# Residual rows of three layer norms and low parts of five weight blocks moved from GpSimd to VectorE, and a selection cut into ten steps

## The chip, the cores and the metric

One core of one Trainium2 chip. The metric is the device time of one execution in microseconds (us), the median of several runs. Engines are named as the profile names them: PE (TensorE matmul), PEld (its weight loads), DVE (VectorE), ACT (ScalarE), POOL (GpSimd), SP (SyncE, which issues all the loads of weights here).

## The reference, cut to what matters

The program runs four transformer layers on 256 tokens of width 1024, all in float32. Layers 0 and 1 (sparse attention, retention, MLP) are not touched by the change. Layers 2 and 3 use post-layer-norm:

```python
def second_block(x, ...):
    for i in range(DEPTH):                     # DEPTH = 2
        h = mixer_sb_ssm(x, ...) if i % 2 == 0 else mixer_dsa(x, ...)
        x = layer_norm(ALPHA * x + h, ln_mix_g[i], ln_mix_b[i])
        x = layer_norm(ALPHA * x + sq_relu_mlp(x, mlp_w1[i], mlp_w2[i]), ln_ffn_g[i], ln_ffn_b[i])

def layer_norm(x, g, b):
    y = (x - mean(x)) * rsqrt(var(x) + 1e-5) * g + b

def mixer_dsa(x, w_in, w_out):                 # "sparse attention" below
    q, k, v, qi, ki, wi = split(x @ w_in)
    score = einsum(relu(qi . ki), wi)          # 8 index heads of 32
    score = where(causal, score, -inf)
    idx = top_k(score, 64)                     # per query
    ... softmax attention over the 64 chosen keys, 16 heads of 64, ALiBi slopes
    return o @ w_out
```

There are four layer norms in layers 2 and 3. The last one writes the output and has other code; the other three are called norm 1 (after the mixer of layer 2), norm 2 (after the MLP of layer 2) and norm 3 (after the sparse attention of layer 3).

## The kernel before, in words

**Split products.** Each float32 product is made of three matmuls: weights and activations are split into a high part (rounded) and a low part (`lo = x - hi`), and `mm3` (lines 378 to 383) sums hi·hi, hi·lo and lo·hi. Weights come in units, one after the other in the list of `_sequence` (line 233), each as two halves of 128x1024 elements a partition row block. For each half SP issues the load into a `raw` buffer, ACT writes `hi` (line 357), and DVE or POOL writes `lo` (line 359): `_split` gives the first `POOL[name]` halves of a unit to POOL and the rest to DVE. `raw`, `hi` and `lo` have five buffers each; in layers 2 and 3 a unit is split one unit ahead of its use.

**The order of the work.** The body is Python that traces instructions in program order. When the kernel is built, a scheduler with its own model of times puts each engine's instructions in a fixed order: of those that are ready in the model, the one traced first goes first. `behind` (line 293) forces what is traced in its block to stand behind given instructions on the same engine, without waiting for their end. Side work is written as generators: `e.add` puts one in a list, and each `yield` of the main work calls `e.step` (line 303), which runs each side generator by one step. So the place of a `yield` decides between which pieces of the main work a piece of side work is traced.

**The layer norm** (`_LayerNorm`). Tokens lie in two tiles T = 0, 1 of 128, columns in two halves. `half` (line 505) makes statistics; `turn` (line 553) transposes the normalised rows on PE, ACT applies gain and bias (line 1576), and `cut` (line 1582) makes the high part on DVE (line 1589) and the low part on POOL for T = 0 (line 1594) and on DVE for T = 1 (line 1591). The next matmuls need these `ah` and `al` tiles. `finish` (line 1601) then traces the residual rows: the normalised activation in row layout, gain and bias applied, which is added again much later (line 1516 in the next norm, or line 2010 in the sparse attention's output). Three quarters of it are made in `finish` on POOL (lines 1611 and 1612): for T = 0 all 1024 columns, for T = 1 the second 512.

**The MLP** (`_mlp`, line 1232) follows norms 1 and 3. Products `f1(c)` (48 matmuls) and the rows of `f2(c)` alternate; for each c, DVE has four `lo`, one square (line 1241) and one low part (line 442).

**The sparse attention** (`_dsa`, line 1874) follows norm 2. In program order: units dki, dqi, dv 0, dv 1 (index keys, index queries, values and index weights), then dk and dq 0 to 3 (keys, queries), of eight k-tiles each; each of these gives two `yield`s. After dk, `put_k` (line 1921) and after each dq, `put_q` (line 1928) copy the result out of PSUM on ACT and DVE (DVE: lines 1926 and 1936). All ten halves of dk and dq have their `lo` on POOL. Side work `side_index` (line 1891) begins at the first yield of dk: it makes the scores of 8 index heads (matmuls line 1896, relu on ACT line 1898, two multiply-adds on DVE line 1902), then eight passes of line 1908 (the eight largest) and line 1910 (strike them out), then the mask `dm` (lines 1912 and 1913), all traced in one step. After it come 18 steps of `_attention` (line 717): `stage_a` (scores on PE lines 743 and 744, DVE line 1956, ACT line 1959, DVE lines 1961 and 1964), `stage_b` (transposes line 1971, ACT line 1973), `stage_c` (line 1985, and low parts at line 442). A step waits until the dq it needs has been traced. In this kernel seven of these steps are traced between the dq units. The output product `do` (96 matmuls of 512 columns) starts once two pairs of heads are done and is interleaved with the rest of the attention; it is completed inside norm 3's `last_rows` (line 1424).

Of the kernel before, what the change touches and what calls it, by code (L numbers as in the profile page):

```python
# [12 lines left out]
ALU = mybir.AluOpType  # L13
# [247 lines left out]
class _Env:  # L261
    BUFS = {"raw": 5, "hi": 5, "lo": 5, "ah": 8, "al": 8, "b8": 5, "b4": 7, "b2": 12, "b1": 7, "sm": 24, "s16": 32,
            "rc": 2}
    AHEAD, LOAD = 2, 4
    POOL = {"dk": 2, "dq": 2, "rv": 1, "rg": 1, "ma": 1, "mb": 1, "up": 1, "su": 1, "glu": 1, "sv": 1, "ksw": 1}

    def __init__(self, ctx, tc, ws):
        self.tc, self.nc, self.ws = tc, tc.nc, ws
        self.pools = {}
        self.ctx = ctx  # L270
        self.ps = {k: ctx.enter_context(tc.tile_pool(name="ps" + k, bufs=4, space=PSUM)) for k in "aw"}
        self.table, _ = _offsets()
        self.seq = _sequence()
        self.pos = {k: n for n, k in enumerate(self.seq)}
        self.raws, self.parts = {}, {}
        self.loaded = self.cut = 0
        self.n = 0
        self.side = []
        self.after = ()
    def t(self, tag, shape, dt=F32):  # L280
        if tag not in self.pools:
            self.pools[tag] = self.ctx.enter_context(
# [19 lines left out]

    def step(self):
        for item in list(self.side):
            with self.behind(item[1]):
                over = next(item[0], self) is self
            if over:
                self.side.remove(item)
# [130 lines left out]
def _hilo(e, hi, lo, src):  # L439

    return (e.nc.scalar.activation(out=hi, in_=src, func=AF.Copy),  # L441
            e.nc.vector.tensor_tensor(out=lo, in0=src, in1=hi.bitcast(F32), op=ALU.subtract))  # L442
# [30 lines left out]
class _Norm(_Act):  # L473
# [8 lines left out]
    def slice(self, xT, c):  # L482
        self.add(xT[:, 2 * c:2 * c + 2], self.g[:, 2 * c:2 * c + 2])
        if c == 0:
            self.e.after = self.last
        self.square(xT, c)
# [745 lines left out]
def _mlp(e, i, act, rows, late=lambda: None):  # L1232

    nc = e.nc
    rels = {}

    def f1(c):
        def emit(_, bank):
            r = e.t("b2", [128, 2, 256])
            nc.scalar.activation(out=r, in_=bank, func=AF.Relu)  # L1240
            nc.vector.tensor_tensor(out=r, in0=r, in1=r, op=ALU.mult)
            h = e.t("b2", [128, 2, 256], F32R)
            l = e.t("b2", [128, 2, 256], F32R)
            _hilo(e, h, l, r)
            rels[c] = ([h[:, 0], h[:, 1]], [l[:, 0], l[:, 1]])
        e.run(e.transposed(("f1", i, c), act, emit, kind="w"))

    e.AHEAD = 1
    f1(0)
    for c in range(13):  # L1250
        f1(c + 1)
        e.run(rows((c,), (rels.pop(c),)))
    late()
    f1(14)
    f1(15)
    e.run(rows((13, 14, 15), (rels[13], rels[14], rels[15])))
# [231 lines left out]
class _LayerNorm:  # L1488

    def __init__(self, e, K, lncol, ln, out, xn, which, i, final):
        self.e, self.K, self.xn, self.final, self.out = e, K, xn, final, out
        self.gb = []
        for v in range(2):
            t = e.t("b4", [128, 1024])
            row = 4 * which + 2 * v + i
            e.nc.sync.dma_start(out=t, in_=ln[row:row + 1, :].to_broadcast([128, 1024]))
            self.gb.append(t)
        self.gc, self.bc = (lncol[:, 8 * (4 * which + 2 * v + i):8 * (4 * which + 2 * v + i) + 8] for v in range(2))  # L1500
        self.xo = e.t("b8", [128, 2, 1024])
        self.v, self.st, self.src = [], [], []
        self.hi, self.lo = [], []
# [49 lines left out]
    def turn(self, T):  # L1553
# [7 lines left out]
        for h in range(2):  # L1561
# [17 lines left out]
            if T == 1:  # L1579
                self.cut(T, h)  # L1580

    def cut(self, T, h):
        e, V, G = self.e, self.e.nc.vector, self.e.nc.gpsimd
        ts = slice(128 * T, 128 * T + 128)
        y = self.y.pop((T, h))
        for n in range(2):
            q = 2 * h + n
            hi, lo = self.hi[q][:, :, ts], self.lo[q][:, :, ts]
            V.tensor_copy(out=hi, in_=y[:, 2 * n:2 * n + 2])  # L1589
            if T:  # L1590
                self.vlast = V.tensor_tensor(out=lo, in0=y[:, 2 * n:2 * n + 2], in1=hi.bitcast(F32), op=ALU.subtract)  # L1591
            else:
                with e.behind((self.pow,)):
                    self.glast = G.tensor_tensor(out=lo, in0=y[:, 2 * n:2 * n + 2], in1=hi.bitcast(F32),
                                                 op=ALU.subtract)
# [5 lines left out]
    def finish(self):  # L1601
        if self.final:
            return
        e, G = self.e, self.e.nc.gpsimd
        self.cut(0, 1)
        e.warm(6, (e.mlast,))
        self.turn(1)
        e.after = (self.alast, self.vlast)
        with e.behind((self.glast,)):
            for T, c in ((0, slice(0, 1024)), (1, slice(512, 1024))):  # L1610
                G.tensor_tensor(out=self.xo[:, T, c], in0=self.v[T][:, c], in1=self.gb[0][:, c], op=ALU.mult)
                G.tensor_tensor(out=self.xo[:, T, c], in0=self.xo[:, T, c], in1=self.gb[1][:, c], op=ALU.add)  # L1612
        l2 = lambda ts: [t[:, k] for t in ts for k in range(2)]
        return self.xo, (l2(self.hi), l2(self.lo))

# [258 lines left out]
def _dsa(e, act, C, ident, mask1, l2, acc, ai, xn):  # L1874
# [16 lines left out]
    def side_index():  # L1891
        for h in range(8):
            hs = slice(32 * (h % 4), 32 * (h % 4) + 32)
            ps = e.bank()
            for T, (o, n) in enumerate(span):
                PE.matmul(out=ps[:, o:o + n], lhsT=qi[hs, h // 4, 128 * T:128 * T + 128], rhs=ki[hs, :n])
            r = e.t("b2", [128, 384])
            A.activation(out=r, in_=ps[:, :384], func=AF.Relu)
            for T, (o, n) in enumerate(span):
                sl = slice(o, o + n)  # L1900
                prev = mask1[:, 256 - n:] if h == 0 else idx[:, sl]
                V.scalar_tensor_tensor(out=idx[:, sl], in0=r[:, sl], scalar=vw[:, T, 256 + h:257 + h], in1=prev,  # L1902
                                       op0=ALU.mult, op1=ALU.add)
        for it in range(8):
            src = work if it else idx
            m8 = [e.t("sm", [128, 8]) for _ in range(2)]
            for T, (o, n) in enumerate(span):
                V.max(out=m8[T], in_=src[:, o:o + n])
            for T, (o, n) in enumerate(span):
                V.match_replace(out=work[:, o:o + n], in_to_replace=m8[T], in_values=src[:, o:o + n],  # L1910
                                imm_value=-3e38)
        V.tensor_tensor(out=dm, in0=work, in1=idx, op=ALU.is_equal)
        V.scalar_tensor_tensor(out=dm, in0=dm, scalar=FAR, in1=C["negd"], op0=ALU.mult, op1=ALU.add)
        yield from _attention(e, 16, stage_a, stage_b, stage_c, 2, lambda s: len(queries) > min(s, 15) // 4)
# [128 lines left out]
```

## Time and profile before

| what | value |
|---|---|
| median of 3 runs | 1530.6 us (1530.14 to 1534.49) |
| the profiled execution, its own time | 1529.34 us |
| its span, first to last instruction | 1527.6 us |
| PE busy | 1460.5 us, 96% of the span |
| DVE busy | 1057.9 us, 69% |
| ACT busy | 772.6 us, 51% |
| POOL busy | 382.2 us, 25% |
| granted PE clock, mean | 0.98 of 2.4 GHz |

How to read it: the busy time of an engine is summed over records; matmuls are pipelined, so their records overlap. PE is the engine to watch: a stretch costs time where PE is idle, or where its granted clock is 0.5 (1.2 GHz in place of 2.4). An idle PE shows in the trace as a wait in square brackets in front of a matmul, with the instruction that ended it. Norm 1 lies at 1020 to 1024 us of the span, norm 2 at 1209 to 1216, norm 3 at 1330 to 1335, the sparse attention between the last two.

### The profile page before, as it was taken

The page shows a single profiled execution, that of the slowest core. Times are in us where ns is not written, and L with a number is a line of the kernel's source. Part 1 is how long each engine was busy: PE and PEld are TensorE (multiplying, and loading weights), DVE is VectorE, ACT ScalarE, POOL GpSimd, SP SyncE. Part 2 cuts the span into 40 slices and gives each one's busy share as a digit, 9 for nine tenths or more (in the row PEclk, how much of TensorE's full clock was granted, in tenths as well). Part 3 has the DMA queues.
Part 4 walks back from the last instruction along what each step waited for, and adds up shares of the span by engine and source line. Part 5 has one row for each costly group of instructions (what it writes and reads, how often), then busy time and mean ns, then how long its engine had stood idle before and what let it go on. Part 6 is the DMA issues. An engine that isn't in the chain of part 4 may idle for free.

```text
span 1527.6 us, 26445 instructions
## 1 busy us (share of the span) xinstructions
PE 1460.5 (96%) x10596; PEld 1334.1 (87%) x10596; DVE 1057.9 (69%) x1628; ACT 772.6 (51%) x1192; POOL 382.2 (25%) x274
## 2 busy tenths in 40 slices
PE   7999999999989999988999999999999888999997
PEld 6868999999988789988999998778999787789997
DVE  7687768555688786699755778876555669675556
ACT  5555445444546554453544555464444447644442
POOL 4353314000144433158200237520000251110000
PEclk8999999999999999998999999999999999999999
DMA  7553455555455554533655453236555352255551
GB/s 247 198 171 119 148 187 166 194 184 188 161 154 196 189 173 139 184 133 125 202 170 186 156 177 125 97 124 206 188 186 189 108 187 97 97 180 191 185 189 69
DMA packets 70682, 250.75 MB, mean 164 GB/s; under 512 B 8096, under 2 KB 8480, under 8 KB 70560
## 3 DMA queue, kind: packets, MB, share of 16 engines
q1 hardware_dynamic: 70560, 249.07, 49.1%
q8 instruction: 83, 1.36, 0.4%
q14 instruction: 39, 0.32, 0.1%
HBM read 247.99 MB, written 1.05 MB: 163 GB/s over the span
## 4 chain that ended last, share of the span: by engine, by line
PE 77%; DVE 13%; issue 3%; ACT 2%; DMA 2%; POOL 1%; DVEq 0%; SPq 0%; ACTq 0%; POOLq 0%
PE psa L382 14%; PE psa L381 14%; PE psa L383 14%; PE psw L382 9%; PE psw L383 9%; PE psw L381 9%; DVE lo L359 3%; DMA raw<-in_ws_dram 2%; DVE al L462 1%; ACT hi L357 1%; DVE al L1591 1%; PE psw L1057 1%; DVE b L1902 1%; DVE b L1851 1%; DVE b L1031 1%
## 5 line engine op out<-in xcount | busy, mean ns | idle before, releaser
L359 DVE TENSOR_TENSOR lo<-raw,hi 128x1024 fp32r<-128x1024 f32 (+2 forms) x397 | 504.3, 1279 | 324.9 <-ACT hi L357 324.5
L357 ACT ACTIVATE hi<-raw 128x1024 fp32r<-128x1024 f32 (+1 forms) x448 | 465.2, 1045 | 505.4 <-PE psw L382 207.1
L382 PE MATMUL psw<-al,hi 128*128 128x256 f32 x1152 | 328.4, 285 | 6.6 <-DVE al L1591 5.5
L383 PE MATMUL psw<-ah,lo 128*128 128x256 f32 x1152 | 328.2, 285 | 3.0 <-DVE lo L359 2.8
L381 PE MATMUL psw<-ah,hi 128*128 128x256 f32 x1152 | 328.0, 285 | 0.0
L382 PEld LDWEIGHTS psw<-al,hi 128*128 128x128 f32 x1152 | 222.8, 193 | 9.2 <-POOL b L1612 4.6
L383 PEld LDWEIGHTS psw<-ah,lo 128*128 128x128 f32 x1152 | 222.7, 193 | 4.1 <-DVE lo L359 4.0
L381 PEld LDWEIGHTS psw<-ah,hi 128*128 128x128 f32 x1152 | 222.5, 193 | 1.1
L382 PE MATMUL psa<-b,hi 128*128 128x256 f32 x640 | 182.4, 286 | 8.5 <-DVE b L442 8.5
L383 PE MATMUL psa<-b,lo 128*128 128x256 f32 x640 | 181.8, 285 | 0.0
L381 PE MATMUL psa<-b,hi 128*128 128x256 f32 x640 | 180.4, 286 | 0.6 <-ACT b L441 0.6
L359 POOL TENSOR_TENSOR lo<-raw,hi 128x1024 fp32r<-128x1024 f32 x51 | 125.1, 2457 | 210.6 <-ACT hi L357 192.2
L381 PE MATMUL psa<-ah,hi 128*128 128x256 f32 x456 | 133.7, 294 | 1.5 <-DVE ah L1589 1.5
L382 PE MATMUL psa<-al,hi 128*128 128x256 f32 x456 | 132.1, 290 | 2.0 <-DVE al L1591 2.0
L383 PE MATMUL psa<-ah,lo 128*128 128x256 f32 x456 | 132.6, 291 | 0.0
L382 PEld LDWEIGHTS psa<-b,hi 128*128 128x128 f32 x640 | 124.1, 194 | 9.3 <-DVE b L442 9.2
L382 PE MATMUL psa<-lo,ah 128*128 128x512 f32 (+2 forms) x320 | 123.1, 387 | 8.1 <-DVE lo L359 7.1
L383 PEld LDWEIGHTS psa<-b,lo 128*128 128x128 f32 x640 | 124.2, 194 | 0.0
L381 PE MATMUL psa<-hi,ah 128*128 128x512 f32 (+2 forms) x320 | 123.5, 394 | 0.5 <-ACT ah L1412 0.4
L381 PEld LDWEIGHTS psa<-b,hi 128*128 128x128 f32 x640 | 123.0, 194 | 1.0 <-ACT b L441 0.9
L383 PE MATMUL psa<-hi,al 128*128 128x512 f32 (+2 forms) x320 | 119.6, 386 | 1.2 <-DVE al L462 1.2
L1526 POOL TENSOR_TENSOR sm<-sm,mhalf 128x1 f32<-128x1 f32 x8 | 5.8, 722 | 449.7 <-DVE sm L1525 445.2
(352 smaller groups left out, 2753.6 us busy)
## 6 DMA issues: line engine op xcount, KB each, us to landing
raw<-in_ws_dram SPq DMA_DIRECT2D x450, 512.0 KB, 4.2
b<-in_ln_dram SPq DMA_DIRECT2D x8, 512.0 KB, 5.1
raw<-in_ws_dram SPq DMA_DIRECT2D x8, 280.0 KB, 4.3
raw<-in_ws_dram SPq DMA_DIRECT2D x4, 264.0 KB, 2.7
b<-in_x_dram SPq DMA_DIRECT2D x4, 256.0 KB, 5.1
out_dram<-b SPq DMA_DIRECT2D x4, 256.0 KB, 2.0
cb<-in_cb_dram SPq DMA_DIRECT2D x1, 676.0 KB, 7.5
b<-in_p_dram SPq DMA_DIRECT2D x2, 256.0 KB, 5.1
```

Source lines behind the costliest of these rows:

```text
L357: self.nc.scalar.activation(out=hi, in_=w, func=AF.Copy)
L359: eng.tensor_tensor(out=lo, in0=w, in1=hi.bitcast(F32), op=ALU.subtract)
L381: mm(out=out, lhsT=lh, rhs=rh, start=start, stop=False, skip_group_check=shared)
L382: mm(out=out, lhsT=lh, rhs=rl, start=False, stop=False, skip_group_check=shared)
L383: self.mlast = mm(out=out, lhsT=ll, rhs=rh, start=False, stop=stop, skip_group_check=shared)
L462: v = e.nc.vector.scalar_tensor_tensor(out=l[:, k], in0=srcs[:, k], scalar=g, in1=h[:, k].bitcast(F32), op0=ALU.mult, op1=ALU.subtract)
L1031: V.tensor_scalar(out=sb[:, o:o + n], in0=sb[:, o:o + n], scalar1=sm[:, T:T + 1], scalar2=None, op0=ALU.mult)
L1057: PE.matmul(out=o[64 * gg:64 * gg + 64, q0:256], lhsT=kvn[:, kt, v0:v0 + 64], rhs=pts[s - 2 + 2 * gg][:, 256 * kt:256 * kt + 256 - q0], st ...
L1526: self.glast = self.pow = G.tensor_tensor(out=r, in0=r, in1=self.K["mhalf"][:, :1], op=ALU.pow)
L1591: self.vlast = V.tensor_tensor(out=lo, in0=y[:, 2 * n:2 * n + 2], in1=hi.bitcast(F32), op=ALU.subtract)
L1851: V.tensor_tensor_scan(out=xs[:, q, c], data0=mt[:, q], data1=w[:, q, c], initial=0.0, op0=ALU.mult, op1=ALU.add)
L1902: V.scalar_tensor_tensor(out=idx[:, sl], in0=r[:, sl], scalar=vw[:, T, 256 + h:257 + h], in1=prev, op0=ALU.mult, op1=ALU.add)
```

## The change

Three parts:

1. The `lo` of dk (2 halves) and dq (8 halves) is made on DVE: `dk` and `dq` leave the `POOL` table.
2. The residual rows of norms 1 to 3 become a side generator on DVE, `rows`: six instructions of 128x512 in each norm, one a step, after a pause of two steps. Each is traced behind the pair of instructions last put in `e.marks`: the norm's last `ah`/`al`, or in an MLP the last high and low part of an `f1`.
3. The selection yields after index heads 3 and 7 and after each of its eight passes: ten steps where there was one.

```diff
-    POOL = {"dk": 2, "dq": 2, "rv": 1, "rg": 1, "ma": 1, "mb": 1, "up": 1, "su": 1, "glu": 1, "sv": 1, "ksw": 1}
+    POOL = {"rv": 1, "rg": 1, "ma": 1, "mb": 1, "up": 1, "su": 1, "glu": 1, "sv": 1, "ksw": 1}
...
     def step(self):
         for item in list(self.side):
-            with self.behind(item[1]):
+            with self.behind(item[1]() if callable(item[1]) else item[1]):
...
 (in _mlp, f1)
-            _hilo(e, h, l, r)
+            e.marks = _hilo(e, h, l, r)
...
 class _LayerNorm:
+    PAUSE = 2
...
+    def rows(self):
+        V = self.e.nc.vector
+        yield from _pause(self.PAUSE)
+        for T, c in ((0, slice(0, 512)), (0, slice(512, 1024)), (1, slice(512, 1024))):
+            V.tensor_tensor(out=self.xo[:, T, c], in0=self.v[T][:, c], in1=self.gb[0][:, c], op=ALU.mult)
+            yield
+            V.tensor_tensor(out=self.xo[:, T, c], in0=self.xo[:, T, c], in1=self.gb[1][:, c], op=ALU.add)
+            yield
...
     def finish(self):
...
-        e.after = (self.alast, self.vlast)
-        with e.behind((self.glast,)):
-            for T, c in ((0, slice(0, 1024)), (1, slice(512, 1024))):
-                G.tensor_tensor(out=self.xo[:, T, c], in0=self.v[T][:, c], in1=self.gb[0][:, c], op=ALU.mult)
-                G.tensor_tensor(out=self.xo[:, T, c], in0=self.xo[:, T, c], in1=self.gb[1][:, c], op=ALU.add)
+        e.after = e.marks = (self.alast, self.vlast)
+        e.add(self.rows(), lambda: e.marks)
...
 (in side_index, head loop)
+            if h in (3, 7):
+                yield
 (in side_index, pass loop)
+            yield
```

## Rows read from the trace of the kernel before

**Rows 1.** The page, part 1: busy us (share of the span) x instructions.
```profile
PE 1460.5 (96%) x10596; PEld 1334.1 (87%) x10596; DVE 1057.9 (69%) x1628; ACT 772.6 (51%) x1192; POOL 382.2 (25%) x274
```

**Rows 2.** Windows, one row a stretch: length, busy us (count) by engine, PEclk, DMA, GB/s.
```profile
1024.30:1042.40 18.10, 15.17 (x110) 14.35 (x109) 16.47 (x16) 9.74 (x15) 8.94 (x6) 0.91 0.36 105
...
1216.20:1232.40 16.20, 12.70 (x77) 12.03 (x76) 11.34 (x11) 6.03 (x11) 7.14 (x4) 0.73 0.36 110
1230.00:1242.50 12.50, 12.50 (x109) 11.78 (x108) 0.71 (x1) 7.29 (x10) 8.91 (x4) 1.00 0.70 243
1257.20:1265.10 7.90, 0.05 (x1) 0.00 (x0) 7.77 (x34) 2.60 (x4) 2.35 (x1) 0.82 0.00 0
1265.10:1269.20 4.10, 4.07 (x19) 4.07 (x20) 3.96 (x17) 2.63 (x5) 2.39 (x1) 0.50 0.40 130
1334.70:1353.00 18.30, 15.20 (x110) 14.39 (x109) 16.52 (x15) 9.66 (x15) 9.11 (x7) 0.91 0.35 113
1360.00:1480.00 120.00, 120.00 (x769) 109.58 (x768) 65.95 (x65) 56.85 (x66) 0.00 (x0) 1.00 0.58 192
```

**Rows 3.** Timeline of DVE after norm 1: start us, us, engine, line, operation.
```profile
1025.44 0.31 DVE L1589 CAST ah<-b 128x256 fp32r<-128x256 f32 x1 [0.46 <-ACT b L1576]
1025.78 2.51 DVE L1591 TENSOR_TENSOR al<-b,ah 128x256 fp32r<-128x256 f32 x1
1028.21 1.37 DVE L1589 CAST ah<-b 128x256 fp32r<-128x256 f32 x1
1029.62 2.46 DVE L1591 TENSOR_TENSOR al<-b,ah 128x256 fp32r<-128x256 f32 x1
...
1039.45 1.23 DVE L359 TENSOR_TENSOR lo<-raw,hi 128x1024 fp32r<-128x1024 f32 x1
1040.60 0.68 DVE L442 TENSOR_TENSOR b<-b,b 128x512 fp32r<-128x512 f32 x1
```

**Rows 4.** Timeline of POOL after norm 1, line L1611 (L1612 follows alike).
```profile
1025.56 3.88 POOL L1611 TENSOR_TENSOR b<-b,b 128x1024 f32<-128x1024 f32 x2
```

**Rows 5.** Waits of PE after norms 1, 2 and 3: us, times, longest.
```profile
PE psw L382 <- DVE al L1591: 2.7, 2, 2.1
...
PE psa L382 <- DVE al L1591: 2.0, 2, 1.1
PE psa L381 <- DVE ah L1589: 1.5, 1, 1.5
...
PE psw L382 <- DVE al L1591: 2.9, 2, 2.1
```

**Rows 6.** Timeline of DVE in the sparse attention: index scores, first pass of the selection.
```profile
1243.00 5.10 DVE L1902 SCALAR_TENSOR_TENSOR b<-b,b,ca 128x128 f32<-128x128 f32 x2 [12.27 <-ACT b L1898]
1248.02 8.99 DVE L1902 SCALAR_TENSOR_TENSOR b<-b,b,b 128x128 f32<-128x128 f32 x14
1256.94 0.61 DVE L1908 MAX8 sm<-b 128x8 f32<-128x128 f32 x2
...
1258.11 0.61 DVE L1908 MAX8 sm<-b 128x8 f32<-128x128 f32 x2
...
1273.32 0.35 DVE L1956 CUSTOM_DVE_ANT_0 b<-psw,b,cb 128x128 f32<-128x128 f32 x1
```

**Rows 7.** Timeline of POOL in the sparse attention.
```profile
1233.59 16.78 POOL L359 TENSOR_TENSOR lo<-raw,hi 128x1024 fp32r<-128x1024 f32 x7 [10.25 <-ACT hi L357]
```

**Rows 8.** Timeline of PE in the sparse attention.
```profile
1256.97 0.28 PE L382 MATMUL psa<-al,hi 128*128 128x256 f32 x1
1265.13 0.47 PE L743 MATMUL psw<-b,b 128*128 128x128 f32 x1 [7.89 <-DVE b L1936]
...
1279.32 0.27 PE L1971 MATMUL psw<-ca,b 128*128 128x128 f32 x1
```

**Rows 9.** Line L1902 by itself: duration ns min/median/max, first and last start.
```profile
L1902 DVE SCALAR_TENSOR_TENSOR b<-b,b,b x14: 339/472/2492, 1248.0 to 1256.5; 128x128 f32<-128x128 f32 x7, 128x256 f32<-128x256 f32 x7
```

**Rows 10.** Groups by line on DVE, 1230 to 1330 us: count, busy us, mean ns, idle before.
```profile
L1936 DVE SCALAR_TENSOR_TENSOR b<-psa,cb,b 64x256 fp32r<-64x256 f32 x16 | 7.7, 483 | 0.5
```

More of the change, by code (lines that the diff above doesn't have):

```diff
@@ L278, in __init__ @@
         self.side = []
-        self.after = ()
+        self.after = self.marks = ()
     def t(self, tag, shape, dt=F32):
@@ L1603, in finish @@
             return
-        e, G = self.e, self.e.nc.gpsimd
+        e = self.e
         self.cut(0, 1)
```

## Prediction

> **What bounds the kernel now.** I read the page first: PE is busy 96% of the span, DVE 69%, POOL 25% [rows 1]. So work moved between DVE and POOL can pay only where PE stands still for it. The next views were the stretches behind the three norms and inside the sparse attention, with busy time and granted clock [rows 2], then the timelines that say what PE waited for.
>
> After norm 1, from 1024.3 to 1042.4 us, PE is busy 15.17 of 18.10 us and the mean granted clock is 0.91 [rows 2]. The waits are for line 1591, the low part for T = 1 [rows 5]. That instruction has 256 elements a row and takes 2.51 and 2.46 us, while one with 512 takes 0.68 [rows 3]. Beside it POOL runs the residual rows, 1.9 us an instruction on average [rows 4]. The starts show the pattern: DVE's low part starts at 1025.78, just behind POOL's at 1025.56, and lasts about as long as the POOL instruction; a cast of 0.31 us becomes 1.37 [rows 3, 4]. So in this trace DVE and POOL take turns, each waiting out the other's whole instruction. PE stands idle for it, and after the idle time comes a stretch at the lower clock (1.2 in place of 2.4 GHz), which brings the mean to 0.91 [rows 2]. Norm 3 shows the same, and norm 2 too, with a wait for the cast of line 1589 besides [rows 2, 5].
>
> In the sparse attention the same happens to the index scores. Sixteen multiply-adds of line 1902 take 5.10 + 8.99 us [rows 6], with single ones at 2.49 us where 0.34 and 0.47 are the undisturbed sizes [rows 9]; POOL is then making `lo` of dk and dq in one run of 16.78 us [rows 7]. The selection ends late, `put_q` stands behind it in DVE's order, and PE waits 7.9 us at the first attention score, with 4.1 us at half clock behind that [rows 2, 8].
>
> **Part 1, residual rows off POOL.** It removes twelve POOL instructions and adds 18 on DVE of 128x512 with two inputs, at 0.68 each [rows 3]: 12.2 us of DVE. They need cover. In an MLP DVE is busy 66 of 120 us [rows 2], so 4.1 us a norm fits in the room of one or two `f1`/`f2` pairs; after norm 2 they follow `vlast` at once and DVE has 11.8 of 12.5 us free before the index scores [rows 2]. I cost them at nothing; without that cover 12.2 us would land on the path. Nothing waits for the rows soon (lines 1516 and 2010 come far later); the gain, bias and `v` buffers are held until they are done, and the next users of that pool come after those 12.5 us.
>
> What it frees: after norm 1 DVE's four instructions take from 1025.44 to 1032.08, 6.6 us; undisturbed I take 0.3 for each cast and 0.4 for each low part (estimate, a little over half the 0.68 of twice the size), 1.4 us. The low parts are then ready before PE reaches them. What PE gets back, norm by norm:
> - Norm 1: lower bound the waits alone, 2.7 us [rows 5]. Upper: the stretch not busy, 18.10 - 15.17 = 2.9, plus the clock, 0.09 x 18.1 = 1.6: 4.6 us. I take 4.5, since the half clock comes right behind the idle that goes.
> - Norm 3: waits 2.9; not busy 3.1 plus 1.6 for the clock: 4.7. I take 4.7.
> - Norm 2: waits 3.5; not busy 3.5 plus 0.27 x 16.2 = 4.4 for the clock: 7.9. Part of that clock loss lies inside the idle time and part before it, so I take 5.5.
> Sum 14.7 us, bounds 9.1 and 17.2. What is late next are the four `lo` behind line 1591; they have their `hi` and start 5 us sooner too.
>
> **Part 2, `lo` of dk and dq on DVE.** POOL loses ten instructions of 2.4 us (16.78 / 7); DVE gains ten at 1.23 us [rows 3, 7]: 12.3 us. Six have their `hi` before the index scores start at 1243.0 and fall in the free 11.8 us together with the rows (7.4 + 4.1 = 11.5); four come later. No transfer is added; on SP the loads of the next units wait for a `raw` buffer, and DVE gives it back sooner.
>
> **Part 3, ten steps.** No instruction is added, only program order. Up to now all of the selection stood ahead of `put_k`, the dq units and their `lo`, which did not matter while POOL made these. Now the `lo` of dq 1 to 3 and the `put_q` come between the passes, and the first seven attention steps come behind dq 3, where they stood between the dq units. Where does the selection end? From 1242.5 DVE has: index scores 8 x (0.34 + 0.47) = 6.5; eight passes at 1.17 (start to start) = 9.4; two instructions of line 1926 at 0.68 = 1.4; the mask 1.1; sixteen of line 1936, 7.7; four `lo`, 4.9 [rows 3, 6, 9, 10]. Sum 31.0: it ends at 1273.5, where the first line 1956 stands today (1273.32). So on this clock the attention starts no earlier. But PE need not wait meanwhile: with all products of dq 2 and dq 3 ahead of the scores it has work through the 7.9 us hole. It gets back 7.9 + half of 4.1 = 9.9 us (upper bound). What it gives back: those products covered the attention's start. Today PE's first transpose (line 1971) comes 6.0 us behind the first line 1956, with `put_q` and `lo` between on DVE [rows 6, 8]; with less of that between I take half, 3 us bare, and then 4.1 us at half clock as now, 2 more. Net 5; upper bound 9.9; lower -4, with the whole 6.0 us bare at the start, again before the first `do` rows, and the clock: 9.9 - 14.
>
> Sum: 14.7 + 5 = 19.7 us. From the profiled execution's 1529.3 that makes 1509.6; the median of the runs lies 1.3 above the profiled one, so I say **1510.5**. A change under 0.3% (4.6 us) cannot be told from none.
>
> A rule speaks against it. DVE's total hardly changes: +12.2 +12.3 us of new work against some 3 x 5.2 = 15.6 us of standing behind POOL after the norms and 14.1 - 6.5 = 7.6 at line 1902 saved [rows 3, 6, 9]. The Trainium skill says in "Perfetto Trace Analysis", section "Optimizing Scalar/DVE Operations", that GpSimd and DVE share an SBUF port, so shifting operations between the two might not help. By that rule the sum is zero, 1530.6; by the rows the saved time lies where PE waits and the new time where DVE is idle.
>
> **The rivals.**
> 1. *The time lost to turns is only exchanged.* DVE's sum of +24.5 and -23.2 decides and PE finds as much to wait for: 1531. For it: DVE is busy 7.77 of the 7.9 us of PE's hole. Against: 11.8 of 12.5 us idle just before [rows 2]. Chance 5%.
> 2. *The attention is laid bare.* The norms give 14.7, but selection or start-up is so late that the sparse attention gains nothing or loses 4: 1514 to 1521. For it: DVE's 31.0 us have little slack, and the first seven steps lose their cover. Chance 17%.
> 3. *All comes back.* Upper bounds everywhere, 17.2 + 9.9: 1503.5. It needs the `do` rows' first matmuls (line 2010) and the scores to fill the start. Chance 12%.
> 4. *Slower: `lo` late for each dq.* In DVE's fixed order the two `lo` of a dq unit stand behind pieces of the selection and `put_q`, which themselves wait for PE. If each of the four dq units then costs PE a wait like today's 7.9 us, that is 31.6 less the 7.9 that goes, +23.7, against 14.7: 1539.6. It decides from 20 us lost on. Against: four to six of eight such `lo` can be done before the index scores. Chance 3%.
> 5. *The change does not take effect*, because the scheduler keeps the rows beside the low parts: then they are DVE instructions between, 0.68 in place of 1.9 each [rows 3, 4]; the norms gain about half, and with the 5 us that is 1518. Chance 3%.
>
> **How the numbers follow.** The forecast has 60%: 1505 to 1516 around 1510.5. Rivals 2 and 3 reach to 1521 and 1502. The range 1502 to 1521 leaves out rivals 1 and 4 and the tails of the others, under 2 in 10. Faster by over 0.3%: the forecast and rivals 2, 3 and 5, 0.92; the same: rival 1, 0.05; slower: rival 4, 0.03.
>
> **What would show it.** Right: lines 1591 and 1589 at 0.4 and 0.3 us and no PE wait for them; PEclk near 1.0 in the 18 us after norms 1 and 3; line 1902 at 0.34 and 0.47; no wait of 7.9 us at line 743, a new one of about 3 us at line 1971 or 743 later. POOL busy down by some 47 us (ten times 2.4, and three norms times two lines at 3.9). Wrong: `lo` of line 359 as releaser of PE in dq 1 to 3, rows of `rows` between `lo` and `al` in an MLP with PE waiting for those, or dm later than 1275 on the old clock less the norms' gain.

## The result, and the profile after

The changed kernel takes **1515.7 us** (median of four runs, 1514.2 to 1516.7) against 1530.4 us for the kernel before beside it: a ratio of 0.990, 95% interval 0.988 to 0.992, so 12 to 19 us faster. The forecast was 1510.5 us, in a range of 1502 to 1521. The profiled execution of the changed kernel took 1516.7 us (span 1514.9), that of before 1529.3.

Lines have shifted: 359 is now 360, 381 to 383 are 382 to 384, 743 and 744 are 744 and 745; 1589, 1591 and 1594 are 1602, 1604 and 1607; 1902, 1908, 1910, 1912, 1913, 1936, 1956 and 1971 are 1912, 1920, 1922, 1925, 1926, 1949, 1969 and 1984; 2010 is 2023. The rows are lines 1590 and 1592. The kernels of the experiments shift some lines a little further: `put_q` is line 1946 in e1, and the softmax's multiplication by a factor per row, 1977 here, is 1974 in e8 and 1981 in e11 and e12.

The page, part 1, and then windows of the same length behind the three norms as in [rows 2], moved so that they begin at the same instruction as there, together with two stretches at the start of the attention (length, busy us and count by engine, PEclk, DMA, GB/s):

```profile
PE 1454.6 (96%) x10596; PEld 1327.8 (88%) x10596; DVE 1055.0 (70%) x1656; ACT 772.4 (51%) x1192; POOL 335.3 (22%) x252
```

```profile
1027.98:1046.08 18.10, 17.98 (x133) 17.04 (x132) 15.18 (x22) 11.75 (x17) 1.30 (x2) 1.00 0.59 204
1214.45:1230.65 16.20, 15.72 (x119) 15.51 (x118) 12.62 (x19) 8.99 (x16) 0.26 (x1) 0.89 0.53 168
1327.15:1345.45 18.30, 18.26 (x134) 17.29 (x133) 15.34 (x22) 11.81 (x17) 1.49 (x3) 1.00 0.59 203
1260.00:1270.00 10.00, 5.54 (x35) 3.91 (x33) 9.65 (x25) 4.15 (x8) 0.00 (x0) 0.97 0.51 170
1270.00:1280.00 10.00, 7.69 (x22) 4.45 (x23) 8.54 (x37) 5.46 (x20) 0.00 (x0) 0.52 0.02 8
```

POOL is 46.9 us less busy and DVE's total is 2.9 us lower, against [rows 1]. After the norms PE's clock is 0.89 to 1.00 where [rows 2] had 0.73 to 0.91. But from 1260 to 1280 there is a hole. DVE behind norm 1, the answer to [rows 3]:

```profile
1029.11 0.32 DVE L1602 CAST ah<-b 128x256 fp32r<-128x256 f32 x1 [0.45 <-ACT b L1579]
1029.46 0.43 DVE L1604 TENSOR_TENSOR al<-b,ah 128x256 fp32r<-128x256 f32 x1
1029.81 0.29 DVE L1602 CAST ah<-b 128x256 fp32r<-128x256 f32 x1
1030.14 0.43 DVE L1604 TENSOR_TENSOR al<-b,ah 128x256 fp32r<-128x256 f32 x1
1030.76 5.87 DVE L360 TENSOR_TENSOR lo<-raw,hi 128x1024 fp32r<-128x1024 f32 x5 [0.19 <-ACT hi L358]
...
1039.97 0.69 DVE L1590 TENSOR_TENSOR b<-b,b 128x512 f32<-128x512 f32 x1
```

The low parts take 0.43 us in place of 2.5, and the first row stands 9 us behind them, inside the MLP, at 0.69 us. PE no longer waits for line 1604. In the sparse attention DVE now reads (to be held against [rows 6, 9]):

```profile
1236.97 2.06 DVE L1912 SCALAR_TENSOR_TENSOR b<-b,b,b 128x128 f32<-128x128 f32 x6
...
1260.17 1.21 DVE L360 TENSOR_TENSOR lo<-raw,hi 128x1024 fp32r<-128x1024 f32 x1
...
1263.12 1.21 DVE L360 TENSOR_TENSOR lo<-raw,hi 128x1024 fp32r<-128x1024 f32 x1
...
1271.38 0.56 DVE L1925 TENSOR_TENSOR b<-b,b 128x384 f32<-128x384 f32 x1
...
1273.18 0.35 DVE L1969 CUSTOM_DVE_ANT_0 b<-psw,b,cb 128x128 f32<-128x128 f32 x1
```

The index scores are undisturbed (2.06 us for six). Yet the first attention instruction stands at 1273.18, as late as in [rows 6], although this stage began earlier. The waits of PE from 1205 to 1330 us, the largest, and the timeline of PE at that place:

```profile
PE psa L2023 <- DVE b L1949: 6.6, 3, 4.4
```

```profile
1263.43 1.02 PE L2023 MATMUL psa<-b,ai 128*128 128x512 f32 x2
1265.97 1.10 PE L2023 MATMUL psa<-b,ai 128*128 128x512 f32 x2 [1.52 <-DVE b L1949]
1271.49 2.04 PE L2023 MATMUL psa<-b,ai 128*128 128x512 f32 x2 [4.43 <-DVE b L1949]
```

The wait of [rows 8] at the first score is gone, and one of the same kind stands behind the scores, where `do` needs the PSUM banks that `put_q` (line 1949) frees.

**Where the gain lies.** In all traces PE issues the same 10596 instructions, so stretches can be cut at the same instruction, counted from 0. Norm 1: from its first transpose (7554) to 7853. Sparse stage: from norm 2's last transpose (8749) to norm 3's first (9422); it holds the wait behind norm 2 too. Norm 3: 9422 to 9716. The column "first attention" is the start of the first attention instruction on DVE, counted from 8749. All in us, worked out from the starts of instructions in one profiled execution each; the medians and ratios come from all runs.

| kernel | norm 1 | sparse stage | norm 3 | first attention | median | ratio, 95% interval |
|---|---|---|---|---|---|---|
| before | 51.0 | 114.0 | 50.6 | 57.2 | | |
| after | 46.1 | 108.2 | 45.4 | 58.8 | 1515.7 | 0.990 (0.988 to 0.992) |
| e1 rows alone | 46.1 | 110.1 | 45.4 | 53.3 | 1517.1 | 0.991 (0.990 to 0.993) |
| e2 `lo` alone | 50.7 | 111.8 | 49.4 | 60.6 | 1527.8 | 0.998 (0.997 to 0.999) |
| e3 `lo` and steps | 50.7 | 111.4 | 50.2 | 63.4 | 1528.0 | 0.999 (0.998 to 1.000) |
| e4 rows and `lo`, no steps | 46.1 | 108.0 | 45.4 | 57.4 | 1514.6 | 0.989 (0.988 to 0.991) |
| e5 rows on GpSimd, earlier | 50.0 | 105.6 | 49.1 | 57.8 | 1524.8 | 0.996 (0.995 to 0.998) |
| e9 rows on GpSimd, last | 51.9 | 107.4 | 49.6 | 59.6 | 1523.2 | 0.995 (0.993 to 0.997) |
| e6 do on GpSimd | 46.1 | 108.0 | 45.5 | 55.0 | 1514.7 | 0.989 (0.988 to 0.991) |
| e7 dq 2, dq 3, do on GpSimd | 46.1 | 106.8 | 45.5 | 56.1 | 1512.4 | 0.989 (0.987 to 0.991) |
| e8 as e7, one step | 46.1 | 108.7 | 45.5 | 45.8 | 1515.4 | 0.990 (0.988 to 0.991) |
| e10 do held back | 46.1 | 112.1 | 45.4 | 53.6 | 1517.2 | 0.991 (0.989 to 0.992) |
| e11 as e10, and GpSimd | 46.1 | 112.1 | 45.5 | 52.6 | 1519.0 | 0.992 (0.990 to 0.994) |
| e12 do held in part, and GpSimd | 46.1 | 113.2 | 45.5 | 55.1 | 1519.0 | 0.992 (0.991 to 0.994) |

The change gives 4.9 + 5.8 + 5.2 = 15.9 us in the three stretches. The 105.6 us of e5 are no gain of the sparse stage: its wait behind norm 2 lies ahead of it, and the stretch from 7853 to 8749 takes 149.1 us there against 144.9 in after. The part ahead of norm 1, which no version touches, took 1018.3 to 1022.3 us over the fourteen profiled executions, 3.7 us more in after's than in before's. That scatter is why the two profiled executions lie only 12.7 us apart; the medians lie 14.7 apart.

### The profile page after: what moved, and what is told of

Same layout as the page of the kernel before. It is cut to its first block, busy times and chain, and to the rows that moved or that the text cites. A ratio compares the mean times of both kernels' runs of the same rounds, so it can differ in the third digit from the quotient of the medians.

```text
span 1514.9 us, 26451 instructions
## 1 busy us (share of the span) xinstructions
PE 1454.6 (96%) x10596; PEld 1327.8 (88%) x10596; DVE 1055.0 (70%) x1656; ACT 772.4 (51%) x1192; POOL 335.3 (22%) x252
## 4 chain that ended last, share of the span: by engine, by line
PE 79%; DVE 12%; issue 3%; ACT 2%; DMA 2%; POOL 1%; SPq 0%; DVEq 0%; ACTq 0%; POOLq 0%
PE psa L382 14%; PE psa L383 14%; PE psa L384 14%; PE psw L383 9%; PE psw L382 9%; PE psw L384 9%; DVE lo L360 4%; DMA raw<-in_ws_dram 2%; DVE al L463 1%; ACT hi L358 1%; PE psw L1058 1%; DVE b L1861 1%; DVE b L1032 1%; DVE s L1663 1%; PE psw L744 1%
## 5 line engine op out<-in xcount | busy, mean ns | idle before, releaser
L360 DVE TENSOR_TENSOR lo<-raw,hi 128x1024 fp32r<-128x1024 f32 (+2 forms) x407 | 514.5, 1272 | 322.1 <-ACT hi L358 321.3
L360 POOL TENSOR_TENSOR lo<-raw,hi 128x1024 fp32r<-128x1024 f32 x41 | 100.8, 2458 | 192.4 <-ACT hi L358 173.5
```

The costliest lines, as they stand in the source:

```text
L360: eng.tensor_tensor(out=lo, in0=w, in1=hi.bitcast(F32), op=ALU.subtract)
```

## The experiments

### The parts one by one

**e1, rows alone.** Diff against the changed kernel:

```diff
-    POOL = {"rv": 1, ...
+    POOL = {"dk": 2, "dq": 2, "rv": 1, ...
-            if h in (3, 7):
-                yield
...
-            yield                       (behind each pass)
```

> Only the residual rows go to VectorE; the weights' low parts stay on GpSimd and the selection is one step, as before. Theory A (the rows on GpSimd held VectorE's casts and low parts behind each norm, and that is all the gain; what the low parts gain in the sparse attention is given back at its start): the three norms give their 15 us, the sparse attention stays as before with its 7.9 us wait for the index scores, so the time is 1514 to 1517 us, that of the whole change within 2 us. Rival B (the steps cost what the low parts give back, so that the two hide each other): also about 1515 us here, but then the low parts without the steps come out near 1506 us. Rival C (VectorE's sum of work decides, its time is only exchanged): 1525 us or more.

Measured: 1517.1 us, a gain of 13.1 us, at the edge of what theory A said. Norms 1 and 3 are those of after to 0.1 us. The hole of before stands where it was (wait of PE, 1205 to 1330 us):

```profile
PE psw L744 <- DVE b L1946: 8.3, 1, 8.3
```

**e2, low parts alone**: the rows go back to GpSimd as in the kernel before, and the steps go.

```diff
-        e.add(self.rows(), lambda: e.marks)
+        with e.behind((self.glast,)):
+            for T, c in ((0, slice(0, 1024)), (1, slice(512, 1024))):
+                G.tensor_tensor(... v * gain ...)
+                G.tensor_tensor(... + bias ...)
```

> Only the low parts of the sparse attention's weights go to VectorE; the rows stay on GpSimd, the selection is one step. The norms lose their gain (1529 to 1531 us without anything in the sparse attention). Theory A (VectorE has to do the low parts of dq and of do before the attention can start, whichever way the selection is cut, so the wait moves and stays as long): 1528 to 1532 us. Rival B (the ten steps are what puts five low parts of do and the last queries ahead of the mask; without them the mask comes early and the attention starts among dq): 1521 to 1525 us. Rival C (low parts of dq late for the matmuls, as VectorE does 15 us of passes in one stretch ahead of them): 1535 us or more, with waits for the low part at the third matmul of dq.

**e3**: the same with the ten steps kept.

> The low parts go to VectorE and the selection is cut in ten steps, as in the change; the rows stay on GpSimd. Theory A: the sparse attention gives 0.9 us, as in the changed kernel's trace, the norms nothing: 1528 to 1531 us. Rival B says the same of this run; it is the run against which the one without steps is read. If this one comes out at 1524 us or less, the rows on VectorE take 4 us or more out of the sparse attention's gain, which neither theory says.

**e4**: the changed kernel without the steps (the second and third cut of e1's diff).

> The change with its rows and low parts on VectorE, but the selection as one step again. Theory A (VectorE's load ahead of the attention decides, and it is the same with and without steps): 1514 to 1518 us. Rival B (the steps put the mask behind five low parts of do; without them VectorE reaches the mask some 6 us earlier): 1507 to 1511 us. Rival C (the undivided 20 us of scores and passes make the low parts of dq late): 1520 us or more, with waits for the low part inside dq 1 and dq 2.

Measured: e2 1527.8, e3 1528.0 and e4 1514.6 us. The low parts are worth 2.4 us without steps, 2.2 with them, and 1.4 when the rows are on VectorE already (1517.1 against 1515.7). The steps are worth nothing that shows: 0.2 us between e2 and e3, and 1.1 the other way between e4 and after, inside the intervals. So theory A holds in the main (e2 came out 0.2 us below its range), and rival B of this round falls: no version reached the 1506 to 1511 or the 1521 to 1525 us that it asked for.

### Is it the running side by side?

**e5** puts the rows on GpSimd, with a one-element instruction ahead that reads the norm's last low part.

```diff
-        e.add(self.rows(), lambda: e.marks)
+        late = self.lo[3][:, 1, 255:256].bitcast(F32)
+        G.tensor_tensor(out=e.t("sm", [128, 1]), in0=late, in1=late, op=ALU.mult)
+        (the rows on GpSimd as in e2, without behind)
```

> The changed kernel, but the rows go back to GpSimd, as two instructions for each half as before, and start only when the last low part of the norm's rows is made on VectorE (a one-element GpSimd instruction reads that part first). Theory A (the rows hurt only by running at the same time as VectorE's casts and low parts behind the norm): casts and low parts stay at 0.3 and 0.4 us with no wait of TensorE for them; the four GpSimd instructions, some 7.7 us, now take turns with the five low parts of the MLP's weights that stand next on VectorE, so part of the wait can move there: 1515 us if the MLP's cover is enough, up to 1527 us (three norms by 4 us) if it is not, with waits for the low part at the third matmul. Rival C (VectorE and GpSimd do not stop each other; the rows on GpSimd are slow for another reason, or their result is late): 1528 us as in the run with the rows on GpSimd, or more, since they start later still, and without waits for low parts.

Measured: 1524.8 us, but not what was meant. The small instruction had no tie to the rows, and they ran ahead of it. GpSimd, then VectorE, at norm 1:

```profile
1023.45 2.35 POOL L1627 TENSOR_TENSOR b<-b,b 128x1024 f32<-128x1024 f32 x1
1025.76 0.64 POOL L1529 TENSOR_TENSOR sm<-sm,mhalf 128x1 f32<-128x1 f32 x1
...
1033.49 1.11 POOL L1624 TENSOR_TENSOR sm<-al 128x1 f32<-128x1 f32 x1 [1.35 <-DVE al L1604]
```

```profile
1024.25 2.31 DVE L1602 CAST ah<-b 128x256 fp32r<-128x256 f32 x4
...
1032.33 0.42 DVE L1604 TENSOR_TENSOR al<-b,ah 128x256 fp32r<-128x256 f32 x1
```

The low parts of line 1604 are back at 0.42 us, and the casts ahead of them, now beside the rows, take 2.31 us for four (0.3 each undisturbed). PE waits 3.5 us at line 1571, the norm's transposes, instead. VectorE is slower where the rows stand, but that is not the only cause here: GpSimd's own small instruction for the norm's statistics (line 1529), which VectorE needs next, stood behind the second row until 1025.76, 2.1 us after its input was ready. So e5 shows the casts held, and leaves open how much of PE's wait is due to that. **e9** ties them: the small instruction writes into each block of the rows first.

```diff
+            G.tensor_tensor(out=self.xo[:, T, c.start:c.start + 1], in0=late, in1=late, op=ALU.mult)
```

> The changed kernel, with the rows on GpSimd as before, but truly behind the norm: a one-element GpSimd instruction that reads the norm's last low part writes into each block of the rows first, so that no row can start sooner (in the earlier run of this kind nothing tied the rows to it, and they ran ahead of it). Theory A (only the running side by side counts): casts and low parts of the norm at 0.3 and 0.4 us without a wait; the rows, some 7.3 us, take turns with the five low parts of the MLP's weights next on VectorE. TensorE uses one of those in about 2.9 us, so five last it 14 us, and 5.9 + 7.3 = 13.2 us is just in time: 1514 to 1519 us. Rival C (rows on GpSimd are slow whatever stands beside them): 1528 us or more.

Measured: 1523.2 us, outside both. VectorE and GpSimd behind norm 1:

```profile
1025.51 0.43 DVE L1604 TENSOR_TENSOR al<-b,ah 128x256 fp32r<-128x256 f32 x1
...
1026.81 11.28 DVE L360 TENSOR_TENSOR lo<-raw,hi 128x1024 fp32r<-128x1024 f32 x5 [0.19 <-ACT hi L358]
```

```profile
1028.04 5.64 POOL L1626 TENSOR_TENSOR b<-b,b 128x1024 f32<-128x1024 f32 x2
1033.64 5.60 POOL L1627 TENSOR_TENSOR b<-b,b 128x1024 f32<-128x1024 f32 x2
```

The norm's own instructions are undisturbed, and the five `lo` behind them take 11.28 us where they took 5.87. The rows take 11.24 us where [rows 4] and their twins took 7.7. PE stands for the fifth:

```profile
1038.15 0.39 PE L384 MATMUL psw<-ah,lo 128*128 128x256 f32 x1 [1.76 <-DVE lo L360]
```

It needed that one at 1036.4, and its granted clock is 0.50 from 1038.9 to 1045.7 us behind the wait, so norm 1 takes 51.9 us. Theory A's mechanism is right; its cover was reckoned too long, since the fifth `lo` is needed when four are used up, 9.6 us behind the start and not 14. Rival C falls: the same rows hurt a different instruction here than before the change. Behind norm 2 of e9 they cost nothing. The nine `lo` beside them last 14.87 us, but PE does not wait for one, and the sparse stage takes 107.4 us, no more than the 108.2 of after:

```profile
1218.99 14.87 DVE L360 TENSOR_TENSOR lo<-raw,hi 128x1024 fp32r<-128x1024 f32 x9 [0.19 <-ACT hi L358]
```

What no run tried is the rows on GpSimd as late as the change has them on VectorE, piece by piece inside the MLP. So how much of e1's 13.1 us needs the other engine, and how much only the later place, stays open.

### Why the sparse attention gave so little

Five low parts of `do` stood ahead of the mask on VectorE, which the forecast had not counted. **e6** moves `do`'s, **e7** those of dq 2 and dq 3 too, **e8** is e7 without steps.

```diff
+    POOL = {"do": 2, "rv": 1, ...                                     (e6)
+    POOL = {("dq", 2): 2, ("dq", 3): 2, "do": 2, "rv": 1, ...         (e7, e8)
-            eng = self.nc.gpsimd if n < self.POOL.get(key[0], 0) else self.nc.vector
+            eng = self.nc.gpsimd if n < self.POOL.get(key, self.POOL.get(key[0], 0)) else self.nc.vector
```

> The changed kernel, with the low parts of do's weights alone on GpSimd; five of them (1.22 us each, 6.1 us) stood ahead of the mask on a VectorE that was busy 9.7 of 10 us. Theory A (VectorE's load ahead of the attention sets its start, and the five low parts of do are what the forecast left out): the first instruction of the attention on VectorE comes some 6 us earlier against the last dq, the wait at the first matmul of do falls from 6.6 us to 2 us or less, the time is 1508 to 1511 us. Rival B (the softmax's chain and the half clock at its start set it, not VectorE's load): 1514 to 1517 us. Rival C (GpSimd's low parts take turns with VectorE's passes and stop them for 2.4 us each): 1520 us or more.

> The changed kernel, with the low parts of dq 2, dq 3 and do on GpSimd: nine of those that stood between the index scores and the mask (11 us of VectorE) leave it. Theory A: the attention starts when dq 3 is through TensorE, TensorE does not stop between 1255 and 1275 us and keeps its full clock; 1505 to 1509 us, 3 us below the run with do alone. Rival B (the chain of the attention's start sets it): 1514 to 1517 us. Rival C (turns with the passes): 1520 us or more, and waits for the low part inside dq 2 and dq 3, as GpSimd takes 2.4 us for one.

> As the run before, and the selection in one step. Theory A: within 2 us of that run, 1504 to 1509 us, since VectorE's load is the same; as the scores and passes now stand ahead of the last queries, the mask is ready among dq 2 and the attention's first heads are interleaved with dq 3, which can be worth another 1 to 2 us. Rival (without steps the queries' parts, which free TensorE's banks, stand behind the scores and passes, and dq stops as it did before the change): 1510 us or more, with a wait of TensorE for the line of the queries (put_q) inside dq.

Measured: 1514.7, 1512.4 and 1515.4 us. Theory A's 6 us did not come. In e6 GpSimd's low parts ran beside the mask (GpSimd, then VectorE):

```profile
1261.41 4.97 POOL L360 TENSOR_TENSOR lo<-raw,hi 128x1024 fp32r<-128x1024 f32 x2 [1.84 <-ACT hi L358]
```

```profile
1251.34 0.43 DVE L1920 MAX8 sm<-b 128x8 f32<-128x256 f32 x1
...
1262.06 2.12 DVE L1925 TENSOR_TENSOR b<-b,b 128x384 f32<-128x384 f32 x1
1264.21 2.58 DVE L1926 SCALAR_TENSOR_TENSOR b<-b,cb 128x384 f32<-128x384 f32 x1
```

The two mask instructions take 4.7 us in place of 1.1 and eat 3.6 of the 6.1 us freed. None of the three expectations named the mask. The attention still begins 3.8 us sooner in the stage (55.0 against 58.8), and the stage gains 0.2 us. What PE waits for is not the attention's first instruction but `put_q` of dq 3, whose last pieces stand behind it in VectorE's order (PE in e6):

```profile
1270.74 2.04 PE L2023 MATMUL psa<-b,ai 128*128 128x512 f32 x2 [7.28 <-DVE b L1949]
```

This wait ended 58.4 us behind norm 2's last transpose, the longest one of after 57.1. e8 begins 13 us sooner and gains nothing, but it has a new cost as well: GpSimd's low parts of `do` ran beside the softmax's multiplication, which takes 0.55 us undisturbed, and PE waited 4.9 us for it:

```profile
1260.23 2.71 DVE L1974 TENSOR_SCALAR b<-b,sm 128x128 f32<-128x128 f32 x2
```

So in these runs the end of the stage did not follow the start of the attention; what an earlier start would give with nothing else slowed, they do not show. e7 paid too, at the index scores (4.21 us for six, 2.06 in after) and at the first mask instruction (2.50 us). Its hole is smaller all the same: from 30 to 75 us behind norm 2's last transpose PE is busy 38.8 us at a mean clock of 0.92, in after 38.2 us at 0.89. What is left in it is no longer VectorE at its limit (1260 to 1270 us of e7):

```profile
1260.00:1270.00 10.00, 4.08 (x10) 1.03 (x8) 6.64 (x24) 7.85 (x18) 7.00 (x3) 0.88 0.42 147
```

VectorE is busy 6.64 us there. Between 1240 and 1290 it waits 3.2 us, in four pieces, for ScalarE's copies of the queries; two of the pieces (1.0 and 1.1 us) are there because the copy stands behind a high part of `do` on ScalarE (1.06 us each). In `put_q` ScalarE's copies and VectorE's instructions alternate, and ScalarE waits for VectorE in its turn, 12.5 us in e7 and nearly as much in after (1235 to 1290 us; us in all, times, longest):

```profile
ACT b L1948 <- DVE b L1949: 11.1, 10, 2.9
```

So the next three cut `do` only behind the last queries: **e10** with low parts on VectorE, **e11** with the GpSimd table of e7, **e12** as e11 with the first block of `do` left where it was.

```diff
+        if key[0] == "dq":
+            ahead = min(ahead, 3 - key[1])                   (e12: 4 - key[1])
... (the loads of `do` are held back in the same way)
+            if c == 3:
+                e.after = (qa, qv)                           (the last two instructions of put_q)
-        block = e.get(("do", 0, c))
+        block = e.get(("do", 0, c), 2 * c)                   (e12: c)
```

> The changed kernel, with do's weights cut only behind the last queries: neither their low parts on VectorE (five, 6.1 us) nor their high parts on ScalarE (1.06 us each, between the queries' copies) stand ahead of the attention, and nothing runs on GpSimd beside the mask. Theory A2 (the attention starts when both VectorE's load and the exchange between ScalarE's and VectorE's instructions for the queries are through): the first attention instruction on VectorE comes 5 to 6 us earlier, the time is 1509 to 1512 us. Rival B (the start is set by the softmax's chain, or the wait moves to do's low parts, which are now made while the attention runs): 1514 to 1517 us.

> As the run before, with the low parts of dq 2, dq 3 and do on GpSimd too; those of dq are through before the mask's two instructions, those of do run beside attention instructions that read PSUM. Theory A2: VectorE is 11 us lighter ahead of the attention than in the changed kernel, the mask takes 0.56 us for each instruction (2.1 to 2.6 us in the two runs where GpSimd made do's low parts beside it), the attention starts as dq 3 leaves TensorE, and the time is 1505 to 1510 us, 2 to 4 us below the run before. Rival B: within 1 us of the run before. Rival D (GpSimd's 2.4 us for a low part make do late): 1 us or more above it, with waits for the low part at do's matmuls.

> Between the run with the low parts of dq 2, dq 3 and do on GpSimd (1512.4 us) and the run in which all of do was held back as well (1519.0 us): the low parts of dq 2, dq 3 and do on GpSimd, the first block of do cut ahead of the attention as in the changed kernel, the other blocks behind the last queries. Theory A2 (VectorE's load, ScalarE's high parts among the queries and GpSimd beside the mask are what is left): the mask's instructions take 0.56 us, the queries' exchange has three high parts fewer (1.06 us each) in it, the first block of do is ready when its matmuls come: 1508 to 1511 us. Rival B2 (the work ahead of the attention and at its start is a fixed sum of ScalarE and VectorE; what is held back stands in the way of the softmax instead): 1512 to 1518 us.

Measured: 1517.2, 1519.0 and 1519.0 us. Theory A2 falls. In e10 the attention begins 5.2 us sooner, the mask is undisturbed, and the stage becomes 3.9 us longer. The wait moved behind the work that had been held back (line 444 makes a high part of the attention's result); the waits of PE from 1205 to 1330 us, then ScalarE, then VectorE:

```profile
PE psa L384 <- ACT ah L444: 4.7, 1, 4.7
```

```profile
1272.53 3.90 ACT L360 ACTIVATE hi<-raw 128x1024 fp32r<-128x1024 f32 x4
```

```profile
1275.56 4.63 DVE L362 TENSOR_TENSOR lo<-raw,hi 128x1024 fp32r<-128x1024 f32 x4
```

Four high parts stand between the exponentials of the first heads on ScalarE, and behind them four low parts stand on VectorE. In e11 and e12 the low parts of `do` run on GpSimd beside the softmax, and its multiplication (line 1981, one input from SBUF and a factor per row) waits them out; PE waits 9.2 us for it in e11 and 5.5 in e12. e12, GpSimd and VectorE:

```profile
1275.57 6.98 POOL L362 TENSOR_TENSOR lo<-raw,hi 128x1024 fp32r<-128x1024 f32 x3 [14.84 <-PE psw L2002]
```

```profile
1279.01 3.69 DVE L1981 TENSOR_SCALAR b<-b,sm 128x128 f32<-128x128 f32 x2
...
1282.82 0.55 DVE L1981 TENSOR_SCALAR b<-b,sm 128x128 f32<-128x128 f32 x2
```

3.69 us for what takes 0.55. In e12 the first mask instruction was held as well (2.51 us), so theory A2's condition was not met there. Rivals B, D and B2 have it: the wait goes to `do`'s parts or to the softmax.

No version lies clearly below the changed kernel: e7 has the lowest median, 1512.4 us, but its interval (0.987 to 0.991) overlaps that of after.

## Why the prediction was right, and where not

**The mechanism: right.** The rows on GpSimd held VectorE's casts and low parts behind the norm. With the rows off GpSimd they take 0.3 and 0.4 us, as named, and in e5 and e9 the slow instructions are again those beside the rows. That it costs time only where PE waits is shown by e9, where the same rows cost 5.8 us behind norm 1 and nothing behind norm 2.

**Norms, 14.7 us: right.** Norm 1 gives 4.9 (forecast 4.5), norm 3 gives 5.2 (4.7), and norm 2 gives 3.9 (5.5), read as the sparse stage of e1 against that of before. Sum 14.0. As a whole the rows alone measure 13.1 us.

**Rows at no cost: right.** Between norm 1's stretch and norm 2's last transpose, 145.5 us before and 144.9 after, nothing was lost in the MLP that now carries the rows of norm 1; norm 3's stretch, whose MLP carries its own, gained in full, and the program behind it takes 146.9 us in both.

**`lo` and steps, net 5 us: wrong.** They give 1.9 us (110.1 to 108.2). What was to come back did: the index scores run at full pace and PE works through the old hole. What was mis-sized is the give-back, 5 us. From 1260 to 1280 us PE is idle for 4.5 + 2.3 us, and the clock of 0.97 and 0.52 costs 0.2 + 3.7 more (busy time by what is missing from 1): 10.6 us, against the 9.9 that the forecast got back from the old hole. Counted alike from 30 to 75 us behind norm 2's last transpose, the hole costs 11.8 us before, 12.3 in e1 and 10.4 in after: it moved, and lost 1.9. The forecast had a new wait of about 3 us at line 1971 or 743; it came as 6.6 us at the first rows of `do`, for `put_q`. The step at which it fell is the list of VectorE's work up to the mask: 31.0 us with **four** `lo`, where nine stand there, as units are split ahead of their use and five halves of `do` fell among them. Five at 1.22 are 6.1 us. From the first index score (1236.31) to the first attention instruction it takes 36.9 us. The named sign came true: the mask is late by the stage's clock, with the first attention instruction 58.8 us behind norm 2's last transpose where 57.2 less norm 2's 5.5 was due.

That the count alone is the cause is not shown, and here the reasoning was too simple. Taking those five away gave the stage 0.2 us (e6) and cost 3.9 (e10), each time with a new cost beside it: the slow mask, or the held-back parts in the softmax's way. That VectorE, ScalarE's copies and high parts, and the softmax are about equally late, so that relieving one shows the next, is the reading that fits these runs; none of them proves it. So it went most of the way to **rival 2**, the attention laid bare (17%), which has the low parts and steps at nothing or a loss of 4 us, where the forecast has a gain of 5 and 1.9 was measured. Rival 2's time, 1514 to 1521, holds the result. The forecast's own 1505 to 1516 holds it by 0.3 us only, and that is the norms' doing. The forecast's last sum is also 0.4 us off: 1509.6 and 1.3 make 1510.9, not 1510.5.

**The rule that exchanging work between DVE and GpSimd might not help** (rival 1; the Trainium skill, "Perfetto Trace Analysis", section "Optimizing Scalar/DVE Operations") does not decide for the rows: they moved, to another engine and a later place, and 13.1 us went, since GpSimd's share had stood where PE waited. It nearly describes the other part: ten `lo` moved for 1.4 to 2.4 us.

What stays open is which chain would have to be shortened to close the last hole. No run shortened ScalarE's share; every one only moved it. Nor did one shorten `put_q`, whose sixteen pairs of a ScalarE and a VectorE instruction stand at the end of PE's longest wait in this stage before the change, in after and in e1, e4, e6 and e7 (4.0 to 8.3 us).

## What to carry to other kernels

When two engines take turns, move the work to a place where nobody waits, not only to another engine: the 12 us of rows cost nothing inside an MLP, and 7 us of them on GpSimd cost 5 us behind a norm. When a queue is costed up to a point, count everything that a look-ahead puts into it, also for units that come later. And before a second hole is filled, see how many engines are late there: here earlier starts moved the wait, and the end by 1.4 us at best (e7).

## What the runs showed that was not expected

**Which instructions take turns.** Beside GpSimd's rows or low parts, VectorE's casts (e5), subtractions (e9), the mask (e6) and the multiplication by a factor per row (e12, 3.69 in place of 0.55 us) were held. The passes of the selection were not (0.43 us for a MAX8 while GpSimd ran in e6 from 1250.01 to 1252.45), nor `put_q`, which reads one input from PSUM (0.49 us at 1250.82). The Trainium skill, "SBUF — State Buffer", section "Who interferes with whom", says this: GpSimd shares a port pair with VectorE, locked for a whole instruction; a VectorE instruction with two SBUF inputs contends with a GpSimd one that reads SBUF, and copies, casts and `tensor_scalar` can, in modes that use both port pairs; one with at most one SBUF input, outside those modes, does not. The traces agree in each of these cases.

**Both engines pay.** In e9 five `lo` and four row instructions together lasted from 1026.81 to 1039.24, 12.4 us. One after the other they are 5 x 1.22 and, undisturbed as [rows 4] never were, 2 x 2.4 and 2 x 1.3 (e5's instructions of 1024 and 512), 13.5 us. Side by side they saved 1.1 us.

**An untouched stretch has its scatter.** The 1020 us ahead of norm 1, TensorE's same 7554 instructions in every version, differed by 4 us between executions. That is twice what the low parts are worth, so a difference of that size is to be read from the stage and from medians, not from two profiles.
